# A two-layer diffusion trunk on one core: gate and output projection weights in tiles of their own, and six gate chunks of the third branch made early

## The chip, the core and the metric

The kernel runs on one core of a Trainium2 chip. The metric is the time of one execution of the whole program on the device, in microseconds (us). The engines are TensorE (PE in the rows), VectorE (DVE), ScalarE (ACT), GpSimd (POOL) and SyncE (SP), whose queue issues nearly all DMAs here; PEld is TensorE's weight load, which runs beside its matmuls. TensorE's clock has two levels here, 1.2 and 2.4 GHz; the granted clock in the rows is a share of the higher.

## The reference

256 latent tokens and 256 context tokens of width 1024 go through two layers. Each layer modulates and normalizes its input, feeds one wide projection to three attention branches that run side by side, merges them by sigmoid gates, and ends with a SwiGLU block (layer 0) or top-2-of-8 experts (layer 1). Cut to what matters here:

```python
mod = silu(c) @ w_ada            # adaLN vectors
h = modulate(rms_norm(x))
p = h @ w_in                     # keys, values, queries | 3 x 1024 gate columns
y_na  = neighbourhood_attention(...)      # branch 0
y_gqa = blocked_attention(...)            # branch 1, grouped queries
y_mla = blocked_attention(...)            # branch 2, multi-head latent attention
g0, g1, g2 = split(sigmoid(p_gate), 3)
m = g0 * (y_na @ w_o_na) + g1 * (y_gqa @ w_o_gqa) + g2 * (y_mla @ w_o_mla)
x = x + ada_gate * (m @ w_out)
```

A gate depends on h alone, so it can be made at any time after the norm. What it multiplies needs the attention of its branch.

## The kernel before

**Number format.** Every float32 operand is split in two fp16 parts, hi and lo, and each product is three matmuls (hi with hi, lo with hi, hi with lo: lines 332, 333, 334, called by `proj` and `up_proj`). A weight tile comes by DMA as 128x2048 float32 into a buffer named raw (`load_raw`, L304, on SP's queue) and is split in pieces of 1024 columns: ScalarE writes wh (L269), then VectorE writes wl (L266). `RAW, WB = 4, 3` gives a ring of four raw buffers and one of three pairs wh, wl. Buffers and DMAs are handed out in the order in which the program is written, so a raw is issued only when the one three or four places before it (the ring's depth) is no longer read.

**The mixer.** All 512 tokens are the columns of a matmul in the first mixer (128x512). A gate chunk is `proj`: 8 blocks of the width by three matmuls, 24 in all, ended by a tanh on ScalarE. Gate (b,d) is chunk d (128 of the 1024 columns) of branch b. `gate0(d)` writes branch 0 into `macc`; `merge0(d)` multiplies it with the branch's output projection; `merge(b,d)` for b = 1, 2 makes the gate (`gt`, L989), then the output projection, then gt x projection (L266) and the sum into macc (L263). `merge(2,d)` also splits macc into mh, ml, the input of `out_proj`. The weights for these lie in tiles `gw1_d` (1536 columns: a gate chunk and four blocks of w_o) and `gw2_d` (1280: a gate chunk and two blocks).

**The order.** Eight pairs of heads give 16 attention units (context and latent). `scores` (L953) is matmuls that end in a softmax: maximum and sums on VectorE (L925 to 932), the exponential on ScalarE (P, L930), a split into pn, and two DMA transposes per head from SP (L937, pt<-pn). `values` (L969) needs these transposes. `weave` sets dense work (keys, queries, gates, merges) between the units by hand: one list `dense` is dealt out evenly over units(2,6), the eight `merge(1,d)` over units(6,8). Then come the eight `merge(2,d)` alone, each followed by one `ada(1)`, while any is left.

**adaLN columns.** `ada(n)` runs n entries of a queue that makes the second half of the modulation: each c loads two raws of 1 MB which TensorE reads directly as float32 (`ada0_sums`, L426, pg<-raw), ScalarE copies the result to `row` (L429), and TensorE turns it to columns (L436). These raws share the ring with the weights. A raw that TensorE reads is free when the last of its matmuls is done; a weight's raw already when it is split.

**Banks.** `pg` has two PSUM banks, `pa` four, `pb` two; proj, up_proj and ada0_sums share pg.

The second mixer (layer 1, `last`) has 256 queries in place of 512 tokens and no context units; its feed-forward part streams expert weights (in_wm).

Of the kernel before, what the change touches and what calls it, by code (L numbers as in the profile page):

```python
# [54 lines left out]
def layer_tiles(i, w_in, w_uq, w_ukv, w_o_na, w_o_gqa, w_o_mla, w_out, w_gu, w_dn):  # L55

    w = w_in[i]
    r = lambda a, n=128: np.arange(a, a + n)
    swap = np.concatenate([np.arange(16, 32), np.arange(0, 16)])
    o_kna, o_vna, o_kg, o_vg, o_ckv, o_kr = 0, 256, 512, 640, 768, 896  # L60
    o_qna, o_qg, o_cq, o_gate = 928, 1184, 1696, 1952
    perm = _perm()
    t = {}
    t["ckv_kg"] = _chunk_tile(w, [r(o_ckv), r(o_kg)])
    t["cq"] = _chunk_tile(w, [r(o_cq), r(o_cq + 128)])
    t["qg0"] = _chunk_tile(w, [o_qg + perm[0], o_qg + perm[1]])
    t["qg1"] = _chunk_tile(w, [o_qg + perm[2], o_qg + perm[3]])
    t["kna"] = _chunk_tile(w, [r(o_kna), r(o_kna + 128)])
    t["qna"] = _chunk_tile(w, [r(o_qna), r(o_qna + 128)])
    wv = _blocks(w[:, np.concatenate([r(o_vna, 256), r(o_vg), r(o_kr, 32)])])  # L70
    t["v0"] = wv[:, :4].reshape(128, -1)
    t["v1"] = wv[:, 4:].reshape(128, -1)
    qc = np.concatenate([np.concatenate([96 * h + np.arange(96), 96 * h + 64 + swap]) for h in range(4)])
    kc = np.concatenate([np.concatenate([128 * h + np.arange(64) for h in range(4)]),
                         np.concatenate([128 * h + 64 + np.arange(64) for h in range(4)])])
    t["up"] = np.concatenate([_blocks(w_uq[i][:, qc]).reshape(128, -1), w_ukv[i][:, kc]], axis=1)
    rows = np.concatenate(perm)
    wo = [w_o_na[i], w_o_gqa[i][rows], w_o_mla[i]]
    for d in range(4):
        t[f"g0_{d}"] = _chunk_tile(w, [r(o_gate + 256 * d), r(o_gate + 256 * d + 128)])  # L80
    t["wo0"] = _chunk_tile(wo[0], [r(128 * d) for d in range(8)])
    for d in range(8):
        for b in (1, 2):
            t[f"gw{b}_{d}"] = np.concatenate([_chunk_tile(w, [r(o_gate + D * b + 128 * d)]),
                                              _chunk_tile(wo[b], [r(128 * d)])], axis=1)
    for j in range(4):
        t[f"wout{j}"] = _chunk_tile(w_out[i], [r(256 * j), r(256 * j + 128)])
    if w_gu is not None:
        for f in range(NF):
            t[f"gu{f}"] = _chunk_tile(w_gu, [r(128 * f), r(FF + 128 * f)])  # L90
        b = _blocks(w_dn)
        for d in range(8):
            for s in range(2):
                t[f"dn{d}_{s}"] = np.ascontiguousarray(
                    b[:, 11 * s:11 * s + 11, 128 * d:128 * d + 128]).reshape(128, -1)
    return t
# [5 lines left out]
def tile_width(name):  # L102
    if name in ("v0", "v1"):
        return 4 * VW
    if name == "up":
        return 1536
    if name.startswith("gw"):
        return 1536 if name[2] == "1" else 1280
    if name.startswith("dn"):
        return 1408  # L110
    return 2048


def stream_names(i):
    n = list(ORDER_IN) + [f"gw{b}_{d}" for b in (1, 2) for d in range(8)]
    n += [f"wout{j}" for j in range(4)]
    if i == 0:
        n += [f"gu{f}" for f in range(NF)] + [f"dn{d}_{s}" for d in range(8) for s in range(2)]
# [131 lines left out]
def trunk(tc, A, out):  # L250
# [31 lines left out]
        src = A[name]  # L282
        return bass.AP(tensor=src.tensor, offset=src.offset + off, ap=[[w, 128], [1, w]])

    RAW, WB = 4, 3
    raw_slots = [(st, "raw", RAW)]
    wb_slots = [(st, "w", WB)]
    turn = {"raw": 0, "wb": 0}
    issued = [None]
# [327 lines left out]
    def mixer(pool, i, ada_q, nrm, nxt, first=None):  # L617
# [182 lines left out]

        gw = {}

        def gate0(d):

            if d % 2 == 0:
                gw[0] = W(f"g0_{d // 2}")
            S.activation(macc[:, d], proj(gw[0], d % 2, qs), AF.Tanh, scale=0.5 * US)

        cnq, qg, km, qm = [], [], [], []

# [172 lines left out]
            stt(macc[:, d], macc[:, d], 1.0, ps, OP.add, OP.mult)  # L983

        def merge(b, d):
            w = W(f"gw{b}_{d}")
            pgt = proj(w, 0, qs)
            g = ft("gt")[:, :nq]
            S.activation(g, pgt, AF.Tanh, scale=0.5 * US)  # L989
            ks = (None, (2, 3, 4, 5), (6, 7))[b]  # L990
            ps = pg()[:, :nq]
            up_proj(ps, w, [1024 + 128 * n for n in range(len(ks))], [pairs[k][2] for k in ks])
            stt(g, g, 1.0, ps, OP.add, OP.mult)
            add(macc[:, d], macc[:, d], g)
            if b == 2:
# [8 lines left out]
        def weave(us, dense):  # L1004
# [3 lines left out]
            for u in range(n + 1):  # L1008
# [16 lines left out]
        prep = [[cq.proj, cq.proj],  # L1025
                [cq.sums, g0.proj, cq.spread, g0.proj],
                [g0.sums, g1.proj, g0.spread, g1.proj, g0.turn],
                [g1.sums, f(gate0, 0), g1.spread, f(gate0, 1), g1.turn],
                [mla_prep, f(gate0, 2)]]
        if not last:  # L1030
            load_biases(0)
        weave(units(0, 2), prep)
        more_pairs()
        dense = [f(mla_keys, 0), f(mla_keys, 1), f(gate0, 3)]
        dense += [f(mla_query, 0), f(mla_query, 1), f(gate0, 4), f(mla_query, 2), f(mla_query, 3), f(mla_values), f(gate0, 5)]
        dense += [f(ada, 2), f(gate0, 6), f(ada, 1), f(gate0, 7), f(ada, 2)] + [f(merge0, d) for d in range(8)]
        dense += [f(ada, 1), f(ada, 2)]
        weave(units(2, 6), [[d] for d in dense])
        weave(units(6, 8), [[f(merge, 1, d)] for d in range(8)])
        for d in range(8):  # L1040
            merge(2, d)
            ada(1)

        def out_proj(ps, w, a, c):
            c = slice(c.start - q0, c.stop - q0)
# [441 lines left out]
```

## Time and profile before

| | before |
|---|---|
| median of 3 runs | 1771.71 us (1768.15 to 1772.93) |
| the profiled execution's own time | 1771.07 us |
| its span, first to last instruction | 1769.0 us |
| mean granted TensorE clock | 0.977 |
| TensorE busy | 1645.9 us, 93% |
| VectorE busy | 1351.2 us, 76% |
| ScalarE busy | 1037.8 us, 59% |
| moved by DMA | 451.93 MB |

Everything below is read from the one profiled execution. Its stages in time: the first mixer to about 420 us, the dense feed-forward to about 860, the second mixer to about 1036, the experts to the end. A window row gives for each engine the busy time and, in brackets, how many instructions; a busy time below the window's length is idle time. A bracket [0.72 <-DVE wl L266] behind a timeline row says how long the engine had been idle before it and what ended that.

### The profile page before, as it was taken

The numbers are of one execution on the slowest core, as the hardware profiler recorded it, in microseconds if no ns is written. First come the engines' busy times: TensorE is split into PE (matmuls) and PEld (weight loads), VectorE is DVE, ScalarE is ACT, GpSimd is POOL, SyncE is SP. The second block draws the span as 40 slices with busy tenths as digits, with TensorE's granted clock in tenths as the row PEclk, the third lists the DMA queues.
The fourth block names the chain that finished last, engine by engine and source line by source line (L and its number), as shares of the span: only waits on it lengthen the run. The fifth ranks groups of instructions, "written<-read, shape, count | busy, mean of one in ns | idle before, by whom it ended". The sixth has DMA issues, their size and how long they took to land. (4 is left out here: it accounts for less than half of the span.)

```text
span 1769.0 us, 37827 instructions
## 1 busy us (share of the span) xinstructions
PE 1645.9 (93%) x16169; PEld 1086.6 (61%) x16169; DVE 1351.2 (76%) x1906; ACT 1037.8 (59%) x1354; POOL 1.3 (0%) x7
## 2 busy tenths in 40 slices
PE   5999889999899999999888998999999989899987
PEld 2554335446644444457655887787868687868674
DVE  4577656455886555537788778999999999999996
ACT  3456546343432232224656558888878888878785
POOL 0000000000000000000000000000000000000000
PEclk9999899999999999999988998999999999999998
DMA  9253488452365545534536787999999999999990
GB/s 390 102 155 91 108 249 225 135 193 96 134 223 195 186 145 177 195 118 137 146 87 138 188 307 305 424 422 423 417 416 391 423 415 421 420 404 397 407 387 26
DMA packets 149920, 451.93 MB, mean 255 GB/s; under 512 B 92144, under 2 KB 95344, under 8 KB 103024
## 3 DMA queue, kind: packets, MB, share of 16 engines
q1 hardware_dynamic: 148768, 448.50, 68.9%
q8 instruction: 128, 2.10, 0.5%
q10 hardware_dynamic: 976, 0.94, 0.2%
q14 instruction: 48, 0.39, 0.1%
HBM read 427.38 MB, written 1.05 MB: 242 GB/s over the span
## 5 line engine op out<-in xcount | busy, mean ns | idle before, releaser
L266 DVE SCALAR_TENSOR_TENSOR wl<-raw,wh 128x2048 f16<-128x2048 f32 (+1 forms) x476 | 817.2, 1737 | 59.1 <-ACT wh L269 51.6
L269 ACT ACTIVATE wh<-raw 128x2048 f16<-128x2048 f32 (+1 forms) x474 | 684.3, 1464 | 270.7 <-PE pa L333 93.9
L334 PEld LDWEIGHTS <-wl 128*128 128x128 f16 x4346 | 427.3, 98 | 175.8 <-DVE wl L266 54.4
L332 PEld LDWEIGHTS <-wh 128*128 128x128 f16 x4346 | 428.3, 99 | 130.8 <-issue 18.0
L333 PEld LDWEIGHTS <-wh 128*128 128x128 f16 x4346 | 427.6, 98 | 116.6 <-issue 10.1
L334 PE MATMUL pa<-xg,wl 128*128 128x96 f16 x2816 | 374.8, 207 | 37.3 <-DVE wl L266 36.8
L332 PE MATMUL pa<-xg,wh 128*128 128x96 f16 x2816 | 373.6, 206 | 0.0
L333 PE MATMUL pa<-xg,wh 128*128 128x96 f16 x2816 | 373.6, 206 | 0.0
L332 PE MATMUL pg<-hh,wh 128*128 128x512 f16 (+1 forms) x512 | 169.6, 332 | 6.0 <-ACT gt L989 2.6
L332 PE MATMUL pa<-hh,wh 128*128 128x512 f16 (+1 forms) x480 | 167.6, 355 | 6.7 <-ACT hh L569 6.7
L333 PE MATMUL pa<-hl,wh 128*128 128x512 f16 (+1 forms) x480 | 169.9, 355 | 1.9 <-DVE hl L266 1.9
L334 PE MATMUL pa<-hh,wl 128*128 128x512 f16 (+1 forms) x480 | 170.0, 355 | 0.0
L334 PE MATMUL pg<-hh,wl 128*128 128x512 f16 (+1 forms) x512 | 169.1, 331 | 0.7 <-DVE wl L266 0.7
L333 PE MATMUL pg<-hl,wh 128*128 128x512 f16 (+1 forms) x512 | 169.4, 331 | 0.0
L1346 PE MATMUL pg<-wl,hdh 128*96 128x512 f16 x352 | 133.4, 379 | 0.5 <-DVE wl L266 0.2
L1347 PE MATMUL pg<-wh,hdl 128*96 128x512 f16 x352 | 133.3, 379 | 0.0
L266 DVE SCALAR_TENSOR_TENSOR scr<-raw,cb 128x1024 f16<-128x1024 f32 x64 | 78.3, 1223 | 71.0 <-DMA raw<-in_ada 69.8
L1345 PE MATMUL pg<-wh,hdh 128*96 128x512 f16 x352 | 132.2, 379 | 0.0
L266 DVE SCALAR_TENSOR_TENSOR pn<-P,sml,pn 128x512 f16<-128x512 f32 (+1 forms) x96 | 60.7, 659 | 32.8 <-ACT pn L269 32.1
L269 ACT ACTIVATE pn<-P,sml 128x512 f16<-128x512 f32 (+1 forms) x96 | 59.0, 647 | 37.6 <-DMA pt<-pn 26.6
L930 ACT ACTIVATE P<-pa,sml 128x512 f32<-128x512 f32 (+1 forms) x96 | 58.1, 612 | 32.2 <-DVE sml L928 22.6
L334 PE MATMUL pg<-dh,wl 128*128 128x512 f16 (+1 forms) x198 | 70.4, 355 | 0.0
(261 smaller groups left out, 1858.1 us busy)
## 6 DMA issues: line engine op xcount, KB each, us to landing
raw<-in_wm SPq DMA_DIRECT2D x264, 1024.0 KB, 8.2
raw<-in_ws SPq DMA_DIRECT2D x52, 1024.0 KB, 4.8
raw<-in_ada SPq DMA_DIRECT2D x48, 1024.0 KB, 5.0
raw<-in_ws SPq DMA_DIRECT2D x18, 768.0 KB, 4.9
raw<-in_ws SPq DMA_DIRECT2D x16, 704.0 KB, 4.1
raw<-in_ws SPq DMA_DIRECT2D x16, 640.0 KB, 4.0
raw<-in_ws SPq DMA_DIRECT2D x4, 832.0 KB, 11.6
xT<-in_xt SPq DMA_DIRECT2D x4, 512.0 KB, 6.2
```

The costliest lines, as they stand in the source:

```text
L266: return V.scalar_tensor_tensor(o, a, s, b, op0=op0, op1=op1, **kw)
L269: h = S.activation(hi, src, AF.Copy, scale=scale)
L332: T.matmul(ps, sh, mh, start=first, stop=False)
L333: T.matmul(ps, sh, ml, start=False, stop=False)
L334: T.matmul(ps, sl, mh, start=False, stop=last)
L930: S.activation(P[t], ps[t], AF.Exp, bias=nb[:, t:t + 1], scale=sc, accum_out=sums[:, t:t + 1])
L1345: T.matmul(py, hdh[:, f], w[0][:, c], start=begin, stop=False)
L1346: T.matmul(py, hdh[:, f], w[1][:, c], start=False, stop=False)
L1347: T.matmul(py, hdl[:, f], w[0][:, c], start=False, stop=end)
```

## The change

Three things.

1. The 16 tiles `gw1_d`, `gw2_d` of a layer become 11 tiles of 2048 columns: four `g1_*` and four `g2_*` with two gate chunks each, `wo1_0`, `wo1_1` with four chunks' output projection of branch 1, and `wo2` with all of branch 2. The bytes are the same. Both mixers use them.
2. `RAW` goes from 4 to 3, and a fourth raw buffer with a tag of its own, `spare`, joins the ring. In the first mixer this spare leaves the ring from before `weave(units(2,6), ...)` until after the last `merge(2,d)`. Its space holds four gate results, two more lie in buffers tagged acc.
3. In the first mixer, gates (2,0) to (2,5) move out of `merge(2,d)` into the dense list: two after the second `mla_query`, two after gate (0,5), two after gate (0,7). The list grows from 25 to 31 entries, so the dealing over the units shifts too. In both mixers gate (0,4) moves from behind `mla_query` 1 to behind `mla_query` 3.

```diff
-    for d in range(8):
-        for b in (1, 2):
-            t[f"gw{b}_{d}"] = np.concatenate([_chunk_tile(w, [r(o_gate + D * b + 128 * d)]),
-                                              _chunk_tile(wo[b], [r(128 * d)])], axis=1)
+    for b in (1, 2):
+        for d in range(4):
+            t[f"g{b}_{d}"] = _chunk_tile(w, [r(o_gate + D * b + 256 * d), r(o_gate + D * b + 256 * d + 128)])
+    for j in range(2):
+        t[f"wo1_{j}"] = _chunk_tile(wo[1], [r(128 * d) for d in range(4 * j, 4 * j + 4)])
+    t["wo2"] = _chunk_tile(wo[2], [r(128 * d) for d in range(8)])
...
-    RAW, WB = 4, 3
-    raw_slots = [(st, "raw", RAW)]
+    RAW, WB = 3, 3
+    spare = (st, "rx", 1)
+    raw_slots = [(st, "raw", RAW), spare]
...
-        def gate0(d):
+        gates, room = {}, []
+
+        def gate(b, d):
+
 
             if d % 2 == 0:
-                gw[0] = W(f"g0_{d // 2}")
-            S.activation(macc[:, d], proj(gw[0], d % 2, qs), AF.Tanh, scale=0.5 * US)
+                gw["g"] = W(f"g{b}_{d // 2}")
+            if b == 0:
+                g = macc[:, d]
+            else:
+                g = gates[b, d] = room.pop(0) if room else ft("gt")[:, :nq]
+            S.activation(g, proj(gw["g"], d % 2, qs), AF.Tanh, scale=0.5 * US)
...
         def merge(b, d):
-            w = W(f"gw{b}_{d}")
-            pgt = proj(w, 0, qs)
-            g = ft("gt")[:, :nq]
-            S.activation(g, pgt, AF.Tanh, scale=0.5 * US)
+            if (b, d) not in gates:
+                gate(b, d)
+            g = gates[b, d]
             ks = (None, (2, 3, 4, 5), (6, 7))[b]
+            per = 8 // len(ks) * 2
+            if d % per == 0:
+                gw["o"] = W(f"wo1_{d // per}" if b == 1 else "wo2")
             ps = pg()[:, :nq]
-            up_proj(ps, w, [1024 + 128 * n for n in range(len(ks))], [pairs[k][2] for k in ks])
+            o = 128 * len(ks) * (d % per)
+            up_proj(ps, gw["o"], [o + 128 * n for n in range(len(ks))], [pairs[k][2] for k in ks])
...
-        dense = [f(mla_keys, 0), f(mla_keys, 1), f(gate0, 3)]
-        dense += [f(mla_query, 0), f(mla_query, 1), f(gate0, 4), f(mla_query, 2), f(mla_query, 3), f(mla_values), f(gate0, 5)]
-        dense += [f(ada, 2), f(gate0, 6), f(ada, 1), f(gate0, 7), f(ada, 2)] + [f(merge0, d) for d in range(8)]
-        dense += [f(ada, 1), f(ada, 2)]
+        early = [] if last else [f(gate, 2, d) for d in range(6)]
+        if not last:
+            raw_slots.remove(spare)
+            rest = st.tile([128, 4, NTOK], FT, tag="rx", bufs=1, name=nm("gts"))
+            room += [st.tile([128, NTOK], FT, tag="acc", bufs=2, name=nm("gt")) for _ in range(2)]
+            room += [rest[:, j] for j in range(4)]
+        dense = [f(mla_keys, 0), f(mla_keys, 1), f(gate, 0, 3), f(mla_query, 0), f(mla_query, 1)] + early[:2]
+        dense += [f(mla_query, 2), f(mla_query, 3), f(gate, 0, 4), f(mla_values), f(gate, 0, 5)] + early[2:4]
+        dense += [f(ada, 2), f(gate, 0, 6), f(ada, 1), f(gate, 0, 7)] + early[4:] + [f(ada, 2)]
+        dense += [f(merge0, d) for d in range(8)] + [f(ada, 1), f(ada, 2)]
...
+        if not last:
+            raw_slots.append(spare)
```

TensorE behind the latent scores of one unit in the first mixer. Before, three score matmuls (pa), then gate (0,4): its weights wh_1707 are those of tile g0_2.

```order
L953 MATMUL pa_1800<-kg_534,qg_1162 128x512
L953 LDWEIGHTS qg_1162
L953 MATMUL pa_1802<-kg_534,qg_1162 128x512
L953 LDWEIGHTS qg_1162
L953 MATMUL pa_1800<-kg_535,qg_1162 128x512
L332 LDWEIGHTS wh_1707
L332 MATMUL pg_1713<-hh_94,wh_1707 128x512
L333 LDWEIGHTS wh_1707
L333 MATMUL pg_1713<-hl_95,wh_1707 128x512
```

Now, at the same unit:

```order
L961 MATMUL pa_1865<-kg_535,qg_1162 128x512
L961 LDWEIGHTS qg_1163
L961 MATMUL pa_1863<-kg_534,qg_1163 128x512
L961 LDWEIGHTS qg_1163
L961 MATMUL pa_1865<-kg_534,qg_1163 128x512
L333 LDWEIGHTS wh_1662
L333 MATMUL pg_1668<-hh_94,wh_1662 128x512
L334 LDWEIGHTS wh_1662
L334 MATMUL pg_1668<-hl_95,wh_1662 128x512
```

The scores run on, and the chunk behind them is gate (2,0) (wh_1662, of g2_0); gate (2,1) follows it, and gate (0,4) stands behind both later queries.

SP's queue where the raws for the first adaLN columns are issued. Before, raw_2009 is the weight tile g0_3 and raw_2167 the first raw of the next adaLN pair; the four raws of the first pair have been issued far ahead. The rows carry the counters that an instruction waits for.

```order
L937 DMA_TRANSPOSE pt_1983<-pn_1984 128x4x128 [waits DMAHW5_49,DMAHW6_49,DVE_49,PE_49]
L937 DMA_TRANSPOSE pt_1983<-pn_1988 128x4x128 [waits DVE_49]
L304 DMA raw_2009<-in_ws 128x2048 [waits PE_49]
L304 DMA raw_2167<-in_ada 128x2048 [waits PE_49]
L937 DMA_TRANSPOSE pt_2000<-pn_2001 128x4x128 [waits DMAHW0_49,DMAHW7_49,DVE_49,PE_49]
L937 DMA_TRANSPOSE pt_2000<-pn_2005 128x4x128 [waits DVE_49]
L304 DMA raw_2173<-in_ada 128x2048 [waits DMAHW1_49]
L304 DMA raw_2188<-in_ada 128x2048 [waits DMAHW2_49]
```

Now:

```order
L945 DMA_TRANSPOSE pt_2038<-pn_2039 128x4x128 [waits DMAHW5_49,DMAHW6_49,DVE_49,PE_49]
L945 DMA_TRANSPOSE pt_2038<-pn_2043 128x4x128 [waits DVE_49]
L305 DMA raw_2118<-in_ada 128x2048 [waits PE_49]
L305 DMA raw_2159<-in_ws 128x2048 [waits DMAHW7_49,PE_49]
L305 DMA raw_2289<-in_ws 128x2048 [waits DMAHW0_49,PE_49]
L945 DMA_TRANSPOSE pt_2055<-pn_2056 128x4x128 [waits DMAHW1_49,DVE_49,PE_49]
L945 DMA_TRANSPOSE pt_2055<-pn_2060 128x4x128 [waits DMAHW2_49,DVE_49]
L945 DMA_TRANSPOSE pt_2220<-pn_2221 128x8x128 [waits DMAHW3_49,DVE_49,PE_49]
```

raw_2118, the fourth raw of that first pair, stands here and waits for TensorE, which has to be done with the first of the four; raw_2159 (g0_3) and raw_2289 (g2_2) wait for TensorE too, and the transposes of a unit (pt_2055) stand behind the three.

TensorE in the first `merge(2,d)` of the first mixer. Before, an output projection (ym, wh_3234 of gw2_0), one c of adaLN (L426), then the next gate chunk (hh, wh_3303 of gw2_1):

```order
L333 LDWEIGHTS wh_3234
L333 MATMUL pg_3267<-ym_677,wh_3234 128x512
L334 LDWEIGHTS wl_3235
L334 MATMUL pg_3267<-ym_676,wl_3235 128x512
L426 MATMUL pg_3280<-raw_3281,c_81 32x512 x4
L426 MATMUL pg_3280<-raw_3287,c_81 32x512 x4
L332 LDWEIGHTS wh_3303
L332 MATMUL pg_3309<-hh_94,wh_3303 128x512
L333 LDWEIGHTS wh_3303
L333 MATMUL pg_3309<-hl_95,wh_3303 128x512
```

Now:

```order
L334 MATMUL pg_3372<-ym_677,wh_3351 128x512
L335 LDWEIGHTS wl_3352
L335 MATMUL pg_3372<-ym_676,wl_3352 128x512
L427 MATMUL pg_3385<-raw_3386,c_81 32x512 x4
L427 MATMUL pg_3385<-raw_3392,c_81 32x512 x4
L333 LDWEIGHTS wh_3351
L333 MATMUL pg_3406<-ym_674,wh_3351 128x512
L334 LDWEIGHTS wh_3351
L334 MATMUL pg_3406<-ym_675,wh_3351 128x512
L335 LDWEIGHTS wl_3352
L335 MATMUL pg_3406<-ym_674,wl_3352 128x512
```

No gate chunk stands between the output projections (wh_3351 is wo2 for all of them) until chunk 6.

## Rows read from the trace of the kernel before

**Rows 1.** The page: engines over the span, and TensorE's granted clock in 40 slices.
```profile
PE 1645.9 (93%) x16169; PEld 1086.6 (61%) x16169; DVE 1351.2 (76%) x1906; ACT 1037.8 (59%) x1354; POOL 1.3 (0%) x7
...
PEclk9999899999999999999988998999999999999998
```

**Rows 2.** Windows by stage: us, busy and count per engine, clock, DMA share, GB/s.
```profile
145.00:255.00 110.00, 97.91 (x592) 44.27 (x591) 72.79 (x176) 63.17 (x144) 0.00 (x0) 0.92 0.54 152
280.00:352.00 72.00, 72.00 (x391) 34.34 (x389) 40.16 (x73) 30.92 (x60) 0.00 (x0) 1.00 0.64 169
352.00:420.00 68.00, 68.00 (x338) 30.41 (x336) 35.87 (x54) 26.50 (x41) 0.42 (x1) 1.00 0.49 174
1070.00:1769.00 699.00, 647.83 (x9942) 522.16 (x9942) 659.42 (x477) 563.25 (x468) 0.00 (x0) 0.99 0.94 383
```

**Rows 3.** Windows: the two stretches on each side of gate (0,5).
```profile
174.30:205.60 31.30, 24.15 (x152) 11.21 (x152) 24.44 (x59) 20.80 (x53) 0.00 (x0) 0.84 0.34 61
205.60:272.00 66.40, 61.78 (x408) 28.60 (x409) 35.53 (x85) 31.92 (x72) 0.00 (x0) 0.97 0.81 246
```

**Rows 4.** Windows of 5 us inside these stretches.
```profile
190.00:195.00 5.00, 2.11 (x14) 0.80 (x13) 4.61 (x10) 2.75 (x6) 0.00 (x0) 0.95 0.61 82
195.00:200.00 5.00, 2.24 (x14) 1.28 (x15) 2.82 (x6) 1.83 (x4) 0.00 (x0) 0.50 0.00 0
200.00:205.00 5.00, 4.60 (x24) 1.99 (x23) 4.70 (x14) 4.70 (x15) 0.00 (x0) 0.53 0.05 12
245.00:250.00 5.00, 4.81 (x15) 1.71 (x15) 3.10 (x9) 2.39 (x10) 0.00 (x0) 0.66 0.62 262
```

**Rows 5.** Waits of TensorE from 145 to 255 us: total, times, longest.
```profile
PE pa L953 <- ACT P L930: 4.2, 3, 2.8
PE pb L969 <- DMA pt<-pn: 2.2, 3, 1.6
PE pg L332 <- ACT r L728: 1.7, 2, 1.4
PE pg L332 <- ACT wh L269: 1.6, 1, 1.6
```

**Rows 6.** Timeline of TensorE: gate (0,5), adaLN columns, gate (0,6).
```profile
205.60 0.38 PE L332 MATMUL pg<-hh,wh 128*128 128x512 f16 x1 [0.31 <-DVE vl L266]
...
210.56 0.38 PE L334 MATMUL pg<-hh,wl 128*128 128x512 f16 x1
210.87 2.76 PE L426 MATMUL pg<-raw,c 128*32 128x512 f32 x18
...
214.54 1.92 PE L426 MATMUL pg<-raw,c 128*32 128x512 f32 x14
...
217.16 1.05 PE L436 MATMUL pb<-cmat,row 128*128 128x2 f32 x8 [0.16 <-ACT row L429]
...
221.88 0.39 PE L334 MATMUL pg<-hh,wl 128*128 128x512 f16 x1 [0.72 <-DVE wl L266]
```

**Rows 7.** DMA issues from 205 to 232 us: count, KB, median us to landing.
```profile
raw<-in_ada SPq DMA_DIRECT2D x4, 1024.0 KB, 6.3
```

**Rows 8.** The same from 232 to 262 us.
```profile
raw<-in_ada SPq DMA_DIRECT2D x4, 1024.0 KB, 9.4
```

**Rows 9.** Groups by line on VectorE, 85 to 420 us: busy, mean ns, idle before.
```profile
L266 DVE SCALAR_TENSOR_TENSOR wl<-raw,wh 128x1024 f16<-128x1024 f32 x39 | 47.2, 1219 | 7.1 <-ACT wh L269 7.0
...
L263 DVE TENSOR_TENSOR macc<-macc,gt 128x512 f32<-128x512 f32 x16 | 11.1, 691 | 0.5
L266 DVE SCALAR_TENSOR_TENSOR gt<-gt,pg 128x512 f32<-128x512 f32 x16 | 11.0, 686 | 40.9 <-PE pg L334 40.8
...
L266 DVE SCALAR_TENSOR_TENSOR mh<-macc,mh 128x512 f16<-128x512 f32 x8 | 5.5, 687 | 2.1 <-ACT mh L269 2.1
```

**Rows 10.** The same on ScalarE.
```profile
L269 ACT ACTIVATE wh<-raw 128x1024 f16<-128x1024 f32 x39 | 40.2, 1050 | 27.2 <-PE pg L333 18.1 <-DMA raw<-in_ws 4.8 <-issue 3.4
```

**Rows 11.** Waits of TensorE in the second mixer, 950 to 1036 us.
```profile
PE pg L332 <- ACT gt L989: 2.6, 1, 2.6
```

More of the change, by code (lines that the diff above doesn't have):

```diff
@@ L106, in tile_width @@
         return 1536
-    if name.startswith("gw"):
-        return 1536 if name[2] == "1" else 1280
     if name.startswith("dn"):
@@ L114, in stream_names @@
 def stream_names(i):
-    n = list(ORDER_IN) + [f"gw{b}_{d}" for b in (1, 2) for d in range(8)]
+    n = list(ORDER_IN) + [f"g{b}_{d}" for b in (1, 2) for d in range(4)] + ["wo1_0", "wo1_1", "wo2"]
     n += [f"wout{j}" for j in range(4)]
@@ L1027, in mixer @@
                 [g0.sums, g1.proj, g0.spread, g1.proj, g0.turn],
-                [g1.sums, f(gate0, 0), g1.spread, f(gate0, 1), g1.turn],
-                [mla_prep, f(gate0, 2)]]
+                [g1.sums, f(gate, 0, 0), g1.spread, f(gate, 0, 1), g1.turn],
+                [mla_prep, f(gate, 0, 2)]]
         if not last:
```

## The prediction

> **What bounds the kernel now.** I read the page first, then windows by stage, then the waits and the timeline of the stages with idle time. The page shows TensorE busy for 93% of the span, and two of its 40 slices with a granted clock of 8 tenths, both in the first mixer [rows 1]. Windows by stage place this. From 145 to 255 us TensorE is busy for 97.91 of 110 us at a mean clock of 0.92, while from 280 to 420 us (the merges of branches 1 and 2, which give up their gates in part) it is busy for all of 72 and all of 68 us [rows 2]. So the change takes TensorE work out of a stage where TensorE is the limit and puts it where TensorE waits. The six gate chunks cost the same anywhere, 24 matmuls that start 0.216 us apart: 5.2 us from the first to the end of the last start [rows 6]. The gain is what idle and slow-clock time the 31 us of moved work fill. The experts from 1070 us on are paced by DMA (0.94 of its engines) and VectorE (659.42 of 699 us) [rows 2]; nothing there changes, and an earlier mixer moves them forward whole.
>
> How much is there to fill? I take two stretches, split at the start of gate (0,5), and count work at full clock as busy time times granted clock [rows 3]. Stretch one, 31.30 us: 24.15 x 0.84 = 20.3 of work, so 11.0 lost. Stretch two, 66.40 us: 61.78 x 0.97 = 59.9 of work, so 6.5 lost. Together 17.5 us is the most that filling can give.
>
> **Stretch one: two more gates ahead of it, gate (0,4) later.** What is waited for here: the exponential P (4.2 us in all from 145 to 255), the transposed pt (2.2), the rotated r of the latent queries (1.7) [rows 5]. All are ends of chains through VectorE, ScalarE and SP's transposes. The windows show the damage: TensorE is busy for 2.11 and 2.24 of 5 us at 190 and 195, and from 195 to 205 the clock is 0.50 to 0.53, the lower of its two levels [rows 4]. The order puts gates (2,0), (2,1) directly behind the latent scores, so these chains get 10.4 us of cover, and gate (0,4) now covers the last query's rotation. Work added on VectorE is one tile split, two pieces of 1.22 us = 2.4 [rows 9]: 24.44 + 2.4 = 26.9 us in a stretch that would then last 31.3 + 10.4 - 7.5 = 34.2, 79% as before (78%), so VectorE doesn't become the limit. Ends: -11.0 (all filled), -3 (only the 2.85 us wait for P is covered, rounded). I take two thirds of the 11.0, **-7.5**, since the waits come one behind another and the last of a chain stays.
>
> **Stretch two: four more gates, a ring of three.** Filled: 6.5 is lost now, made of the wait for wh of 1.6 [rows 5], 0.72 for wl [rows 6], waits for pt and row, and a slow-clock piece (0.66 at 245 us [rows 4]). With four gates among them I take half, -3.2, between 0 and -6.5.
>
> Against it: with the spare out, an adaLN raw no longer has a slot ahead of time. The four raws of a double step cost TensorE 2.76 + 1.92 = 4.7 us in 18 + 14 records, 1.2 each [rows 6]. Before, all four were loaded far ahead; in the order now, the fourth raw waits until TensorE has read the first. Between lie two raws (2.4), six score matmuls (6 x 0.216 = 1.3) and a column step (some 0.5): 4.2 us of cover. A 1 MB adaLN raw lands 6.3 us after issue in this stretch [rows 7], so TensorE waits for 0 to 2.1 us, there and at two later places (the last raw of the next two double steps). The upper bound is the stretch where several were in flight, 9.4 us [rows 8], or 5.2 of waiting each. I take 1.0 each, **+3.0**, since fewer raws are in flight at a time. Behind that raw on SP stand g0_3, g2_2 and two transposes (pt), which wait too; the values that need them come behind the late raw's matmuls anyway. The tiles that get their slot late (g0_3, wo0, g1_0) cost a wait for a split at two places, as wl does now with 0.72 [rows 6]: +1.3, between 0 and +3.2 (twice the wh wait of 1.6 [rows 5]). The column step behind its row copy waits for 0.16 now [rows 6]; with exponentials queued ahead on ScalarE I take 0.4 at two places, +0.8 (0 to 2). A stall there brings one slow-clock piece like that at 245 us, 5 x (1 - 0.66) = +1.6 [rows 4] (0 to 4.8). Sum: 3.0 + 1.3 + 0.8 + 1.6 - 3.2 = **+3.5**.
>
> A rule that speaks against the change: after the idle window at 190 us the granted clock falls to 0.50 [rows 4]. The Trainium skill, page "TensorE: Matmul & The Clock Gate", section "HAM oscillation — how this bites in real kernels", says that bursts of matmuls with a DMA wait between them start at the low clock again after each wait. The trace agrees for the one wait at 190. By it all three waits for a raw would bring a slow piece, 4.8 in place of 1.6, and the sum below would be 0. [...]
>
> **Merges of branch 2.** Chunks 0 to 5 keep only an output projection, 6 x 0.216 = 1.3 us on TensorE [rows 6], while VectorE has gt, macc and mh, 0.69 + 0.69 + 0.69 = 2.06 [rows 9]. Over six chunks that is 12.4 on VectorE against 7.8 on TensorE plus the four adaLN raws between them (4.8) and two column steps (1.0): 13.6. They nearly balance, and TensorE waits little: **+0.8**, between 0 and +4.6 (12.4 - 7.8, if the adaLN work comes too late to cover). The raws there wait for each other in the ring as well; this lies in the same range.
>
> **Regrouping alone.** Per layer 8 x 1536 + 8 x 1280 columns are 11 x 2048, the same; 32 pieces become 22 of 1024. Ten pieces fewer save at most 10 x 1.22 us on VectorE and 10 x 1.05 on ScalarE [rows 9, 10], and at least nothing. In the merges it is hidden, since TensorE is busy for all of 72 and 68 us [rows 2]: **0** here. In the second mixer, where TensorE does wait, the first merge of branch 1 needs two tiles of 1 MB in place of one of 0.75, and gate (0,4) moves. TensorE's one big wait there is 2.6 us on a gate's tanh [rows 11]; I take **0**, between -2.5 and +2.5.
>
> **Sum.** -7.5 + 3.5 + 0.8 + 0 + 0 = -3.2 us against the profiled execution's 1771.07: **1767.9**. That execution is 0.6 below the median of 1771.71, so this is 0.2% below the median. A measurement of this kernel tells about 0.3% (5.3 us) from no change, so the forecast is "within".
>
> **Rivals.** (A) The gates fill both stretches and a ring of three costs nothing because SP issues early enough: -9 in stretch one, -2 in two, 0 after: about 1760. For it: the waits are chains that 10.4 us of cover outlast, and the forecast's ring waits rest on one landing time. Against it: the order shows the raws waiting for TensorE. (B) Slower: the raw that is issued late lands as in the crowded stretch, 9.4 us [rows 8], so TensorE stands for 5.2 at three places, 15.6 in place of 3.0, and the clock falls each time (+4.8 in place of 1.6): -3.2 + 12.6 + 3.2 = +12.6, about 1784. It passes +0.3% when the three waits are 4 us each, a landing of 8.2. Against it: 9.4 is the median while four raws were queued, and the ring now allows three. (C) The change doesn't do what it says: the waits are not short of work but ends of chains through VectorE (4.61 of 5 us busy at 190 [rows 4]), and the idle time reappears behind the inserted gates. Then stretch one gives -3, the rest +3.5: about 1771.5. (D) VectorE becomes the limit in the merges: +4.6 in place of 0.8, about 1771.7; same side as C.
>
> **Chances.** Forecast 0.46 (1763.5 to 1772.5, a quarter of it under the bound of 1766.4), A 0.28, C and D together 0.16, B 0.10. Faster: 0.28 + 0.12 = 0.40. Slower: B and a little of D, 0.11. Within: 0.49. The range leaves out the outer part of A and of B: 1758 to 1777.
>
> **What would show it.** Right: in the profile after, the windows around 190 to 205 are full at clock 1.00, and waits of L426 on DMA raw appear, about three of 1 us. The merges show TensorE nearly full with VectorE just behind. Wrong: no wait of L426 at all (A), waits of 4 us or more there with clock 0.5 behind (B), waits for P and pt of the same size at a later place (C), or TensorE in the merges waiting for a bank of pg behind VectorE (D). A second mixer that changed by more than 2.5 us would show that the regrouping matters.

## Result and profile after

The changed kernel takes 1784.3 us (median of 7 runs, 1777.4 to 1786.86) against 1771.43 for the kernel before (7 runs, 1768.15 to 1774.82): a ratio of 1.0068, interval 1.0048 to 1.0087. It is slower by about 12 us, where 1767.9 was forecast, and lies outside the range of 1758 to 1777. The profiled executions differ by 10.1 us (1781.09 and 1771.07); what is told below explains these, and the 2 to 3 us by which the medians differ beyond that stay open.

The page of the changed kernel, the lines that answer to [rows 1]:

```profile
PE 1649.3 (93%) x16169; PEld 1086.3 (61%) x16169; DVE 1348.7 (76%) x1886; ACT 1034.8 (58%) x1334; POOL 1.3 (0%) x7
...
PEclk9999999999999999999988998999999999999998
```

TensorE has 3.4 us more of busy time with the same number of matmuls; the first mixer alone has 3.9 more (330.01 before, 333.90 after). Over the whole program the clock doesn't explain it: the mean granted clock is 0.977 in both executions.

Stage lengths tell more. They are differences between the starts of the same instructions in each timeline: the first local scores (pa<-kna,qna; 88.82 us before, 88.88 after), the sums of the norm behind each mixer and behind the dense feed-forward (pb<-cmat,acc; 432.85, 789.55, 1048.91 before, 440.46, 795.49, 1059.62 after), and the span's end.

| us | first mixer, from the local scores | dense feed-forward | second mixer | the rest |
|---|---|---|---|---|
| before | 344.03 | 356.70 | 259.36 | 720.09 |
| after | 351.58 | 355.03 | 264.13 | 719.48 |
| difference | +7.55 | -1.67 | +4.77 | -0.61 |

With +0.06 ahead of the local scores this is the 10.1 us by which the spans differ (1779.1 and 1769.0). Two stages lose, and one of them, the second mixer, has no early gates at all.

Windows of the changed kernel. The first row is stretch one with two gates more (gate (0,5) starts at 209.91 now), the second is stretch two and the first 1.2 us of gate (1,0), the first gate of branch 1; the third and fourth answer to the last two of [rows 2]:

```profile
174.30:209.90 35.60, 31.32 (x199) 14.50 (x197) 28.40 (x60) 23.81 (x54) 0.00 (x0) 1.00 0.42 104
209.90:309.60 99.70, 89.19 (x525) 40.80 (x524) 44.18 (x106) 41.27 (x91) 0.00 (x0) 0.94 0.68 206
352.00:420.00 68.00, 67.43 (x356) 30.40 (x355) 39.34 (x61) 25.08 (x41) 0.42 (x1) 1.00 0.54 184
1070.00:1769.00 699.00, 652.33 (x10000) 525.01 (x9997) 666.13 (x518) 570.66 (x482) 0.00 (x0) 0.99 0.94 386
```

Stretch one holds 10.4 us more of work and is 35.6 - 31.3 = 4.3 us longer, so it gained 6.1. The clock, 0.84 before [rows 3], is 1.00. Stretch two ran from 205.60 to 272.32 before (66.7); now gate (1,0) starts at 308.41, after 98.5 us, of which four gates are 20.7: 77.8, so it lost 11.1. Its idle time is 99.7 - 89.2 = 10.5 us (4.6 before), and its clock 0.94 (0.97 before [rows 3]). The start of gate (1,0), before and after:

```profile
272.32 0.39 PE L332 MATMUL pg<-hh,wh 128*128 128x512 f16 x1
```

```profile
308.41 0.61 PE L333 MATMUL pg<-hh,wh 128*128 128x512 f16 x1 [1.45 <-ACT wh L269]
```

The third row shows TensorE still nearly full from the last merges of branch 1 on (67.43 of 68 us), the fourth the experts paced as before, by DMA at 0.94 and VectorE (666.13 of 699 us).

Windows of 5 us of the changed kernel; the first two answer to [rows 4]:

```profile
190.00:195.00 5.00, 5.00 (x41) 2.73 (x40) 1.81 (x5) 2.94 (x6) 0.00 (x0) 1.00 0.77 154
195.00:200.00 5.00, 3.63 (x18) 1.45 (x17) 4.85 (x8) 2.79 (x5) 0.00 (x0) 1.00 0.23 52
230.00:235.00 5.00, 3.19 (x28) 0.97 (x25) 2.11 (x7) 2.52 (x8) 0.00 (x0) 1.00 1.01 424
235.00:240.00 5.00, 4.88 (x36) 3.76 (x36) 1.64 (x8) 2.85 (x7) 0.00 (x0) 0.55 0.16 62
265.00:270.00 5.00, 4.55 (x34) 1.67 (x29) 0.92 (x3) 0.59 (x1) 0.00 (x0) 1.00 0.76 279
270.00:275.00 5.00, 3.95 (x39) 2.59 (x37) 1.66 (x8) 4.35 (x11) 0.00 (x0) 1.00 0.83 351
290.00:295.00 5.00, 3.28 (x34) 1.76 (x38) 1.96 (x4) 1.55 (x4) 0.00 (x0) 1.00 0.48 106
300.00:305.00 5.00, 3.04 (x19) 1.57 (x16) 1.59 (x5) 0.59 (x1) 0.00 (x0) 0.87 1.01 375
305.00:310.00 5.00, 3.33 (x18) 1.62 (x19) 2.55 (x6) 2.97 (x4) 0.00 (x0) 0.50 0.88 374
```

The idle slice at 190 us is gone; at 195 TensorE is busy for 3.63 of 5 us, and the clock is 1.00 in both. New idle slices stand at 230, 270, 290, 300 and 305. Behind the one at 230 the clock falls to 0.55, and it is at 0.50 from 305 on. Behind those at 270 and 290 it stays at 1.00.

Waits of TensorE in stretch two of the changed kernel, to be held against [rows 5]: total, times, longest.

```profile
PE pb L977 <- DMA pt<-pn: 2.8, 2, 2.6
PE pg L427 <- DMA raw<-in_ada: 2.2, 3, 1.3
PE pa L961 <- ACT P L938: 1.9, 4, 0.7
PE pb L437 <- ACT row L430: 1.8, 3, 0.7
PE pg L333 <- ACT wh L269: 1.4, 1, 1.4
```

Before, in stretch two (205.6 to 272.3 us):

```profile
PE pg L332 <- ACT wh L269: 1.6, 1, 1.6
PE pb L969 <- DMA pt<-pn: 1.5, 1, 1.5
PE pg L334 <- DVE wl L266: 0.7, 1, 0.7
PE pb L436 <- ACT row L429: 0.4, 2, 0.3
PE pa L953 <- ACT P L930: 0.4, 1, 0.4
PE pg L332 <- DVE vl L266: 0.3, 1, 0.3
```

The waits on raw are three, as forecast, and 2.2 us in sum. The larger part is others: transposed softmaxes, exponentials, the row copies, the first tile of branch 1 (1.4, where wh and wl of other tiles cost 1.6 and 0.7 before).

In the second mixer the waits on a gate's tanh double: a wait of 2.6 to 2.8 us is there in both, and shorter ones are new. Before and after, from the projection of branch 1 to the end of the merges:

```profile
PE pg L332 <- ACT gt L989: 2.6, 1, 2.6
```

```profile
PE pg L333 <- ACT gt L815: 5.0, 5, 2.8
```

### The profile page after: what moved, and what is told of

The parts are those of the page before. It is cut to its first block, busy times and chain, and to the rows that moved or that the text cites. A ratio compares the mean times of both kernels' runs of the same rounds, so it can differ in the third digit from the quotient of the medians.

```text
span 1779.1 us, 37737 instructions
## 1 busy us (share of the span) xinstructions
PE 1649.3 (93%) x16169; PEld 1086.3 (61%) x16169; DVE 1348.7 (76%) x1886; ACT 1034.8 (58%) x1334; POOL 1.3 (0%) x7
## 3 DMA queue, kind: packets, MB, share of 16 engines
HBM read 427.38 MB, written 1.05 MB: 241 GB/s over the span
## 6 DMA issues: line engine op xcount, KB each, us to landing
raw<-in_ws SPq DMA_DIRECT2D x4, 832.0 KB, 11.2
```

## Experiments

Stage lengths as above for every kernel, from one profiled execution each; the medians stand in the text. In the second row is a further execution of the kernel before. Two other pairs show how far the same code differs: e10's first mixer is e1's (346.42 and 347.68), e6's is e4's (343.49 and 343.13). So a difference of about 1.3 us in one stage tells nothing by itself.

| kernel | before the local scores | first mixer | dense feed-forward | second mixer |
|---|---|---|---|---|
| before | 88.82 | 344.03 | 356.70 | 259.36 |
| e8_before | 88.25 | 343.61 | 356.72 | 259.85 |
| after | 88.88 | 351.58 | 355.03 | 264.13 |
| e1_regroup | 93.61 | 347.68 | 355.27 | 265.17 |
| e2_ring3 | 93.20 | 351.03 | 355.30 | 258.71 |
| e3_early2 | 93.29 | 345.75 | 355.04 | 267.35 |
| e4_early4_ring4 | 89.40 | 343.13 | 355.69 | 265.70 |
| e5_early4_ring3 | 90.63 | 352.82 | 355.71 | 265.49 |
| e6_old2 | 92.84 | 343.49 | 355.56 | 259.42 |
| e7_old12 | 89.05 | 340.99 | 355.05 | 258.06 |
| e9_early5 | 93.22 | 339.45 | 355.94 | 261.18 |
| e10_step512 | 88.47 | 346.42 | 355.51 | 260.27 |
| e11_poolq | 94.24 | 356.20 | 355.05 | 264.62 |
| e12_ring3_noada | 92.76 | 339.67 | 363.76 | 260.50 |

The stretch ahead of the local scores is the same code everywhere but in e11, which loads its adaLN raws by another queue. It differs by up to 5.4 us even so (88.25 to 93.61; the last section says why), which is why stages are compared and not spans.

**Only the tiles.** The change with no early gate, gate (0,4) in its old place, the ring of four throughout:

```diff
-        early = [] if last else [f(gate, 2, d) for d in range(6)]
+        early = []
-    RAW, WB = 3, 3
-    spare = (st, "rx", 1)
-    raw_slots = [(st, "raw", RAW), spare]
+    RAW, WB = 4, 3
+    raw_slots = [(st, "raw", RAW)]
```

> Only the tiles are regrouped; no gate is moved, the ring has four buffers throughout. Theory (lumps: two 1.05 us splits stand ahead of a gate's tanh on ScalarE where a gate chunk is only 2.6 us long): the first mixer as before within 1.5 us, the second mixer 3 to 5 us longer, so +3 to +6 in all. Rival (the second mixer's loss comes from gate (0,4) standing behind the queries): both mixers as before, total within 1.5 us of before.

Measured: 1779.24 us, ratio 1.0050 (1.0032 to 1.0068). The second mixer is 5.8 us longer, a little more than the 3 to 5 expected; that the first would stay within 1.5 us was wrong, it is 3.7 longer (2.4 in e10, the other execution of the same first mixer). Gate (0,4) stands where it stood, so the rival for the second mixer falls. In the first mixer of this execution the longest new wait is one on a tanh. ScalarE and then TensorE of this kernel:

```profile
290.93 0.72 ACT L269 ACTIVATE pn<-P,sml 128x512 f16<-128x512 f32 x1 [0.48 <-ACT P L937]
296.00 0.72 ACT L269 ACTIVATE pn<-P,sml 128x512 f16<-128x512 f32 x1 [4.34 <-DMA pt<-pn]
296.63 0.58 ACT L814 ACTIVATE gt<-pg 128x512 f32<-128x512 f32 x1
```

```profile
297.25 0.38 PE L332 MATMUL pg<-hh,wh 128*128 128x512 f16 x1 [2.47 <-ACT gt L814]
```

ScalarE sits idle for 4.34 us on a softmax's pn, whose buffer the transposes still read, with gate (1,1)'s tanh behind it in its queue; that tanh frees the bank of pg that gate (1,2) needs, and TensorE waits 2.47. In e10 the order is the same, but the pn waits for 2.66 us and TensorE for 0.79, so how much this order costs differs from execution to execution. Before, the tanh of gate (1,1) stood ahead of that pn:

```profile
286.30 0.59 ACT L989 ACTIVATE gt<-pg 128x512 f32<-128x512 f32 x1
289.35 0.72 ACT L269 ACTIVATE pn<-P,sml 128x512 f16<-128x512 f32 x1 [1.74 <-DMA pt<-pn]
```

With the larger tiles the order in ScalarE's queue is another; that the shifted splits made it so is likely, but not shown.

**Only the ring.** The kernel before with three buffers and a spare, as in the change, and the spare out of the ring in the woven part:

```diff
+        if not last:
+            raw_slots.remove(spare)
         dense = [f(mla_keys, 0), f(mla_keys, 1), f(gate0, 3)]
...
             ada(1)
+        if not last:
+            raw_slots.append(spare)
```

> The kernel before with the ring of raw buffers cut to three from the first woven dense list to the last merge of the first mixer, nothing else. Theory (the ring makes the loss of the second stretch): TensorE's idle time between 205 and 310 us grows by 7 to 11 us, waits of L426 on raw and of values on pt appear, total +7 to +11. Rival (the loss comes from where the early gates put the softmax chains, and three buffers are enough): at most +2.

Measured: 1781.0 us, ratio 1.0060 (1.0040 to 1.0080). The first mixer is 7.0 us longer, the second as before. TensorE's idle time between 205 and 310 us grows from 4.9 to 11.2, by 6.2 where 7 to 11 was expected. The theory holds in kind, a little under its size: of the 10.6 us that the median rose, the stages of the profiled execution show 4.8 behind the start of the local scores, and 4.4 more is the late start of that execution. Waits of TensorE from 205 to 295 us:

```profile
PE pg L427 <- DMA raw<-in_ada: 5.9, 3, 2.7
PE pa L954 <- ACT P L931: 2.8, 1, 2.8
PE pg L333 <- ACT wh L269: 2.6, 1, 2.6
```

**Two early gates, ring of four.**

```diff
-    RAW, WB = 3, 3
...
+    RAW, WB = 4, 3
...
-        early = [] if last else [f(gate, 2, d) for d in range(6)]
+        early = [] if last else [f(gate, 2, d) for d in range(2)]
...
-            raw_slots.remove(spare)
```

> The changed kernel with two early gates in place of six (both stored in the acc buffers) and so with the ring of four. Theory (ring): the first stretch keeps its gain of 6 us, the second stretch loses at most 1, the second mixer keeps its 4.8 us loss: -3 to +1 in all, the first mixer 5 us shorter than before. Rival (crowding by the shifted dense list): the second stretch still loses 4 us or more, the total is +3 or above.

Measured: 1779.38 us, ratio 1.0044 (1.0029 to 1.0060). The expectation missed: the first mixer is 1.9 us shorter than with the tiles alone (345.75 against 347.68), but 1.7 longer than before, and the second is 8.0 longer. Stretch one gained 1.7 us in place of the 6 that were expected, stretch two lost 0.8, within its expected 1, and from gate (1,0) to the norm it is 2.6 longer, where the tiles had been sized at nothing. So the rival's total came, but not by its reason (stretch two).

**Four early gates, ring of four.** Two half-precision results lie in each acc buffer, which changes the gates' rounding, and the product with the projection goes to a tile of its own:

```diff
+            y = ft("gt")[:, :nq] if b == 2 and d < 4 and not last else g
...
+            for _ in range(2):
+                two = st.tile([128, 2, NTOK], F16, tag="acc", bufs=2, name=nm("gt"))
+                room += [two[:, 0], two[:, 1]]
```

> Four early gates, kept in half precision in the acc buffers, with the ring of four. Theory (ring): first mixer 4 to 7 us shorter than before, total -3 to +1. Rival (crowding): the first mixer no shorter than before, total +3 to +8.

Measured: 1775.96 us, ratio 1.0030 (1.0013 to 1.0048). The first mixer is 4.6 us shorter than with the tiles alone in e1 (3.3 against e10) and 0.9 shorter than before. So early gates do gain, and the tiles and the ring take it back. In size the expected 4 to 7 us against before was wrong: stretch one gained 2.3 and stretch two 2.8, but from gate (1,0) to the norm 4.2 is lost.

**The same four with the ring of three**, stored as in the change:

```diff
-        early = [] if last else [f(gate, 2, d) for d in range(6)]
+        early = [] if last else [f(gate, 2, d) for d in range(4)]
```

> The changed kernel with four early gates in place of six: the pair to e4_early4_ring4, with the ring of three. Theory (the costs add: regrouping +3.7 us in the first mixer, ring of three +7.0, four early gates -4.6): the first mixer 6 us longer than before, 7 us longer than e4, with waits on raw of 2 us or more in sum; total +10 to +13. Rival (the ring cost 7 us only in the order of before, since early gates cover the raws): within 2 us of e4.

Measured: 1791.72 us, ratio 1.0120 (1.0094 to 1.0147). The first mixer is 9.7 us longer than with the ring of four, and 8.8 longer than before, where the sum of the single costs (343.61 to 344.03, +3.7, +7.0, -4.6) gives 6: in these executions early gates make the ring's cost larger, not smaller. The 20.6 us by which the median rose are far more than the 10 to 13 expected; the profiled execution shows 14.0 of them behind the start of the local scores. The waits on raw are 1.1 us in sum where 2 or more were expected; the loss shows at the row copies (4.6) and others. The pair differs in how the gates are stored, too, so the 9.7 are the ring's only in the main.

**Old tiles again, part by part.** With four early gates and the ring of four: the second mixer with `gw1_d`, `gw2_d` and its old order (e6, `return i == 1`), and branch 1 of the first mixer too (e7, shown):

```diff
+def old_tiles(i, b):
+    return i == 1 or b == 1
```

> As e4_early4_ring4, but the second mixer has its old tiles and its old order. Theory (the regrouped tiles alone make the second mixer longer): the second mixer back at 259 to 260 us, the first as in e4, total -2 to +1 against before. Rival (the second mixer got longer by where it starts, after another first mixer): still 264 us or more, total +4.

> As e6_old2, and branch 1 of the first mixer has its old tiles too, so that only branch 2 of the first mixer is regrouped, with four early gates and the ring of four. Theory (the 3.7 us that regrouping costs in the first mixer is one wait of gate (1,2) of branch 1 behind ScalarE): first mixer 3 to 5 us shorter than before, total -3 to -6. Rival (that cost comes from branch 2's tiles): as e6_old2, -2 to +1.

Measured: e6 1771.23 us, ratio 1.0001 (0.9985 to 1.0018), the second mixer 259.42; e7 1769.11 us, ratio 0.9991 (0.9977 to 1.0006), the first mixer 2.5 us shorter than e6 (2.1 against e4) and 3.0 shorter than before; its total is 2.0 below before, not the 3 to 6 expected. With e1, where the order is the old one, the second mixer's loss is the tiles' alone: with the old tiles it takes 258.06 to 261.18 us in seven profiled executions, with the new ones, split as in the change, 264.13 to 267.35 in six. From branch 2's first output projection to the norm the seven take 41.25 to 41.62 us, the six 44.45 to 44.61. In the first mixer 2.1 to 2.5 us are branch 1's tiles.

**The kernel before again.**

> The kernel before once more, for how much its stages differ between executions. Theory (the start and the dense feed-forward vary by themselves): from the first local scores on, each mixer within 0.5 us of the first profile; the start up to 5 us and the dense feed-forward up to 2 us apart. Rival (the 1 to 2 us that the dense feed-forward is shorter in all changed kernels is an effect of the changes): 356.7 us again.

Measured: 1769.53 us. Both mixers within 0.5 us. The dense feed-forward is 356.72 again, so the theory falls in that part: it is 0.8 to 1.7 us shorter with every other first mixer but e12's, even with the ring alone. Why is open.

**Five early gates** on top of e7, the fifth result in half precision in 1 KB of its own:

```diff
-        early = [] if last else [f(gate, 2, d) for d in range(4)]
+        early = [] if last else [f(gate, 2, d) for d in range(5)]
+            room += [st.tile([128, NTOK], F16, tag="g5", bufs=1, name=nm("gt"))]
```

> As e7_old12 with a fifth early gate (its half-precision result in 1 KB of its own). Theory (each early gate with the ring of four gives about 1.1 us until the idle time is used up): first mixer 0 to 1.5 us shorter than e7, total -2 to -4 against before. Rival (the fifth gate gives nothing, since its place has no idle time left and merge (2,4) has less cover): as e7 or 1 us longer.

Measured: 1765.94 us, ratio 0.9965 (0.9952 to 0.9979), 5.1 us below before where 2 to 4 was expected, and below both kernels. The first mixer is 4.6 us shorter than before and 1.5 shorter than e7's, about as expected. The price is the half-precision gate. Its waits from 145 to 445 us have none on a raw, and P is at 2.6 in place of 4.2 [rows 5]:

```profile
PE pb L992 <- DMA pt<-pn: 2.7, 2, 2.4
PE pg L348 <- ACT r L744: 2.7, 2, 1.5
PE pa L976 <- ACT P L953: 2.6, 3, 1.1
```

**Smaller split pieces.** e1 with the second mixer's merge tiles split in pieces of 512:

```diff
+            n5 = last and name[:2] in ("g1", "g2", "wo") and name != "wo0"
-            r = load_w(f"ws{i}", offs[name], tile_width(name))
+            r = split_w(load_raw(f"ws{i}", offs[name], tile_width(name)), tile_width(name), step=512 if n5 else 1024)
```

> As e1_regroup, but the second mixer's regrouped tiles are split in pieces of 512 columns in place of 1024. Theory (a 1.05 us split ahead of the tanh holds the gate's bank): the waits of 0.7 us on gt in the merges of branch 2 fall to 0.3 or less and the second mixer gets 1 to 3 us shorter than e1's 265.2. Rival (ScalarE and VectorE have too much to do there in sum, and twice as many pieces cost more): the same or longer by up to 3 us.

The lump in the changed kernel (e1 has the same three waits of 0.70): ScalarE splits 1024 columns while gate (2,1) ends, its tanh comes after, and TensorE waits 0.70 for the bank (three times in this stage):

```profile
1018.58 1.06 ACT L269 ACTIVATE wh<-raw 128x1024 f16<-128x1024 f32 x1
1019.54 0.37 ACT L815 ACTIVATE gt<-pg 128x256 f32<-128x256 f32 x1
```

```profile
1019.96 0.27 PE L333 MATMUL pg<-hh,wh 128*128 128x256 f16 x1 [0.70 <-ACT gt L815]
```

The same place with pieces of 512 (the first columns of e10's rows: start and duration):

```profile
1011.73 0.63 ACT L269 ACTIVATE wh<-raw 128x512 f16<-128x512 f32 x1
1012.26 0.36 ACT L815 ACTIVATE gt<-pg 128x256 f32<-128x256 f32 x1
```

```profile
1012.68 0.27 PE L332 MATMUL pg<-hh,wh 128*128 128x256 f16 x1 [0.27 <-ACT gt L815]
```

Measured: 1775.42 us, ratio 1.0026 (1.0013 to 1.0039); the second mixer is 4.9 us shorter than e1's, where 1 to 3 was expected. The 0.70 became 0.20 to 0.28, as expected; from the first output projection of branch 2 to the norm this is 1.7 us (42.7 against 44.5 us; 41.25 before). The other 3 us come from earlier in the mixer: up to the first output projection of branch 1 it is 4.1 shorter, in branch 1's merges 0.9 longer, with waits on gt of up to 2.0 us. So the lump is shown for the merges of branch 2, and only argued for the rest.

**The adaLN raws on GpSimd's queue**, in the changed kernel:

```diff
-        nc.sync.dma_start(raw[:, :w], dram(name, off, w))
+        (nc.gpsimd if name == "ada0" else nc.sync).dma_start(raw[:, :w], dram(name, off, w))
```

> The changed kernel with the adaLN raws issued from GpSimd's queue, so that no transpose stands behind a raw that waits for TensorE. Theory (part of the ring's cost is SP's queue: transposes behind waiting raws): the 2.6 us wait on pt before 292 us vanishes, the first mixer is 2 to 4 us shorter than the changed kernel's. Rival (the raws are late by their slots, whoever issues them): within 1 us of it.

Measured: 1792.68 us, ratio 1.0129 (1.0110 to 1.0147), the first mixer 4.6 us longer still. The longest wait on pt is 1.5 us in place of 2.6, and stretch two is 2.4 shorter than the change's, but stretch one is 3.4 longer and what follows gate (1,0) 3.6. More is lost on weights and tanh:

```profile
PE pg L333 <- ACT wh L269: 4.9, 3, 3.3
PE pb L437 <- ACT row L430: 3.0, 2, 2.2
PE pg L333 <- ACT gt L815: 2.7, 1, 2.7
PE pb L977 <- DMA pt<-pn: 2.5, 2, 1.5
```

The expectation of 2 to 4 us less for the mixer missed. The move changed more than the one queue position (TensorE waits 4.9 us for weights, 1.4 in the change), so it doesn't tell how much of the ring's cost is transposes behind waiting raws; that stays open.

**The ring of three without the adaLN steps** in the woven part:

```diff
-        dense += [f(ada, 2), f(gate0, 6), f(ada, 1), f(gate0, 7), f(ada, 2)] + [f(merge0, d) for d in range(8)]
-        dense += [f(ada, 1), f(ada, 2)]
+        dense += [f(gate0, 6), f(gate0, 7)] + [f(merge0, d) for d in range(8)]
```

> As e2_ring3, but the adaLN steps are taken out of the woven list (they run between and behind the merges of branch 2 instead). In the kernel before these steps are 14.1 us of matmuls on raws and 6 column steps of about 1 us: 20 us. From the first local scores to the first projection of branch 1 the kernel before takes 188.7 us, so 168.7 is left without them. Theory (the ring of three costs what it does because TensorE itself reads the adaLN raws and frees them late): 167 to 171 us there, no waits of matmuls on wh above 1 us. Rival (three buffers are too few for the weight tiles as well): 173 us or more there.

Measured: 169.26 us from the local scores to the first projection of branch 1 (pg<-qg, at 262.02), within 0.6 of the 168.7 that are left without those steps. Waits of TensorE from 205 to 265 us:

```profile
PE pb L970 <- DMA pt<-pn: 4.6, 5, 1.7
PE pg L333 <- DVE vl L266: 1.1, 1, 1.1
PE pa L954 <- ACT P L931: 0.8, 1, 0.8
```

None on wh. So in this one execution three buffers are enough for the weights as long as no adaLN raws stand among them. That the ring costs what it does because TensorE itself reads those raws fits, and so do the waits on raw in e2 (5.9 us); but e12 takes the raws out of the queue altogether, and the same order with four buffers wasn't run (168.7 is an estimate), so raws that merely crowd the ring are not ruled out. The steps themselves moved later: the dense feed-forward is 7 us longer, the total 1778.71 us.

## Why the prediction was wrong

The first mixer's stretches against the kernel before, with the gates moved into it taken off at 5.18 us each:

| us | stretch one | stretch two | gate (1,0) to the norm |
|---|---|---|---|
| after | -6.1 | +11.1 | +2.6 |
| e1, tiles alone | +0.4 | -0.4 | +3.6 |
| e2, ring alone | +0.3 | +6.0 | +0.7 |
| e4, four gates, ring of four | -2.3 | -2.8 | +4.2 |
| e5, four gates, ring of three | -1.9 | +8.3 | +2.4 |
| e9, five gates, ring of four, branch 1's old tiles | -5.8 | +1.1 | +0.2 |

- **What bounds the kernel: right. The gain of stretch one: nearly right, in part by luck.** -7.5 forecast, -6.1 measured; the window at 190 is full, and the clock is 1.00 throughout. But the same two gates ahead of stretch one gain only 1.7 to 2.3 us in e3 to e7. Their lists of 27 and 29 entries are dealt so that gate (0,4) starts behind the scores of the next unit, and TensorE waits 2.45 to 3.48 us for r ahead of it (1.37 in the change); e9, with 30 entries, gains 5.8. The prediction says nothing of the dealing, which the six gates happened to shift well. That the dealing makes the difference is argued: e11, dealt as the change, gains only 2.7. In e4:

```profile
200.79 0.38 PE L332 MATMUL pg<-hh,wh 128*128 128x512 f16 x1 [2.49 <-ACT r L728]
```

- **Stretch two: the term that failed.** +3.5 forecast, +11.1 measured, and e2 shows that the ring alone, without any early gate, costs 6.0 there. The waits on raw were sized well (2.2 in sum against 3.0: the three raws landed 4.8, 4.8 and 5.4 us after issue, the prediction took 6.3 from [rows 7]). What failed is the rest of the term, which let the others that wait in the same ring and queues off lightly: the row copies cost 1.8 in place of 0.4 before, and P 1.9 in place of 0.4; pt is at 2.8, where half of its 1.5 was to be filled. The late tiles were not worse than forecast: 1.4 at one place, for 2.3 at two before. All idle time grew by 5.9 us. The slow-clock loss is 89.19 x 0.06 = 5.4 us against 62 x 0.03 = 1.9, 3.5 more, where +1.6 was allowed. These two are 9.4 of the 11.1. And the -3.2 for filling never came. With a ring of four it does come: two gates in this stretch make it 2.8 shorter (e4), and with three buffers the same order is 8.3 longer (e5). The order takes a share as well: in e9, ordered nearly as the change, a ring of four still leaves +1.1. That this is because the gates stand in blocks of two and three, behind which the softmax chains and the adaLN steps meet, is argued, not shown.
- **The clock rule that spoke against the change** was nearer than the forecast: 4.8 by it, 1.6 forecast, 3.5 measured. After the idle slices at 230 and 300 us, with raw waits of 0.51 and 1.26, the granted clock is 0.55 and 0.50; after 265 to 275, with a raw wait of 0.45, and after 290, with a wait for pt of 2.6, it stays at 1.00. The Trainium skill, page "TensorE: Matmul & The Clock Gate", section "HAM oscillation — how this bites in real kernels", tells of a kernel whose matmuls start at the low clock again after every DMA wait. The trace agrees for two places of four.
- **Merges of branch 2: right.** +0.8 forecast. From gate (2,0) at 343.89 to the norm at 432.85 it was 88.96; now 381.38 to 440.46 is 59.08, with the six gates' 31.1 it is 90.2: +1.2.
- **Regrouping at 0: the other failed term.** "Hidden, since TensorE is busy for all of 72 and 68 us" looked at instruction counts and not at what stands ahead of what. e1 puts it at +3.7 in the first mixer (+2.4 in e10) and +5.8 in the second, in the change itself it is up to +1.4 from gate (1,0) to the end of branch 1's merges (71.57 to 72.97) and +4.8. TensorE has the two banks of pg for gates and projections; a tanh that comes late behind a split or a pn stopped it for 0.7 us (the change) and 2.5 (e1). The second mixer's bound of 2.5 was taken from the one wait that was there [rows 11], which is no bound for new ones.
- **The rivals.** B had the right sign and nearly the time (1784), but by 15.6 us of waits on raw, which are 2.2: its time is luck. A was wrong: raws do wait. C was wrong in the main, since the early gates gain 3.3 to 4.6 us where the ring stays at four (e4 against e10 and e1), and right in part: in e3 to e7 waits for r do reappear behind the inserted gates, and stretch one gains less than its 3. D did not happen: waits on VectorE in the merges of branch 2 are 0.5 us.
- **Slips in the sums.** Two thirds of 11.0 are 7.3, not 7.5; 5 x (1 - 0.66) is 1.7, not 1.6. A column step is 1.05 us in [rows 6], not some 0.5, so the cover in front of the fourth raw is nearer to 4.7 than to 4.2. C leaves out the +0.8 of the merges: 1772.4. None of them would have brought the forecast near the result.

The parts give -6.1 + 11.1 + 1.4 + 1.2 = +7.6 for the first mixer (measured 7.55), +4.8 for the second, and -1.7 and -0.6 elsewhere.

## What to carry to other kernels

A buffer taken from a shared ring can cost more than what it makes room for gains: here 6 to 11 us in one stretch. Look at who frees its slots last: weight tiles alone, freed once they are split, did with three (e12), and with tiles among them that TensorE itself reads they did not. When DMAs are merged into larger tiles, look not at the instruction count but at the queue of the engine that prepares them: each piece may now stand in front of a small operation that frees a bank. Filling work gained here only where its storage and its tiles left the rest as it was; test storage, tiles and order each alone. And a list that is dealt out by its length changes everywhere when an entry is added: the same two gates gained 2 or 6 us.

## What the runs showed of the hardware

The start of the program differs between executions with the same instructions there. The first two adaLN steps on TensorE in the kernel before and in e1:

```profile
16.46 3.64 PE L426 MATMUL pg<-raw,c 128*32 128x512 f32 x16
...
21.79 1.92 PE L426 MATMUL pg<-raw,c 128*32 128x512 f32 x16
```

```profile
16.98 3.64 PE L426 MATMUL pg<-raw,c 128*32 128x512 f32 x16
...
23.12 3.64 PE L426 MATMUL pg<-raw,c 128*32 128x512 f32 x16
```

Sixteen records take 3.64 us in the first step of both; in the second 1.92 us in the one and again 3.64 in the other, nearly twice as long, while the granted clock from 16 to 25 us reads 1.00 in both. That reading says nothing: the trace's clock records begin only at 20.4 us in the one and at 39.3 in the other, both with a granted clock of 1.00, and ahead of its first record a view prints 1.00 for want of one. The first record lies between the two steps in the kernel before, and behind both in e1. So the steps of 3.64 us ran at the lower level, and the start's length goes by when TensorE first gets the higher one. The other profiles agree: with a first record at 19.4 to 21.2 us the local scores start at 88.25 to 89.40, at 25.3 (e5) at 90.63, and at 38.2 to 39.3 at 92.76 to 93.61 (e11, with its other queue, is left aside). Why the higher level comes late in some executions stays open.

This start can be a good part of the spread between runs of one kernel (1766.84 to 1776.06 us in 18 runs of before), though both profiled executions of that kernel started early; and it is as large as what was looked for.
